# Two edits to a transformer kernel: the head norms' eps add goes from GpSimd to VectorE, and ScalarE writes the high halves of h's first two feature tiles from PSUM

## The chip, the cores and the metric

The kernel runs on one core of a Trainium2 chip. Five engines work side by side, each through its own list of instructions in the order in which they were issued: TensorE (PE, matrix products into the accumulators in PSUM), VectorE (DVE), ScalarE (ACT), GpSimd (POOL) and SyncE (SP, which starts the DMAs). An instruction that needs another engine's result waits for a semaphore, and everything behind it in its engine's list waits too. The metric is the device time of one execution in microseconds (us).

## The reference, cut to what matters

Two transformer models in a row run over 256 tokens of width 1024, two layers each. In the first, a layer is attention (stick-breaking in one, with a forget gate in the other) and a feed-forward net with a width-3 convolution. In the second, layer 0 is differential attention over the tokens and a context of 256 more, layer 1 a short convolution, each with a SwiGLU net. Between any two sub-layers stands the same pattern:

```python
x = x + gate * rmsnorm(o, g_post)             # first model; x + gate * o in the second
h = rmsnorm(x, g_pre) * (1.0 + scale) + shift
y = h @ w                                     # the next sub-layer's first products
```

and in the differential attention each head's queries, keys and outputs are normed once more:

```python
q = rmsnorm_2(q.reshape(bsz, -1, 2, DIFF_HEADS, HEAD_DIM_2), q_norm)
k = rmsnorm_2(k.reshape(bsz, -1, 2, DIFF_HEADS, HEAD_DIM_2), k_norm)
o = rmsnorm_2(o, subln) * (1.0 - lam_init)
# rmsnorm_2(x, g) = x * rsqrt(mean(x * x) + 1e-6) * g
```

## The kernel before, in words

All products are float32 made of pieces: a factor A is split into H (A rounded to the PE's fast float32 format) and L = A − H, and `mm3` makes each product of three matmuls, high·high, low·high and high·low. Weights stream from HBM in pieces of 128x1024; ScalarE casts each to `wh` and VectorE subtracts to get `wl`. The 256 tokens are two token tiles t of 128, the 1024 features eight feature tiles kt of 128.

At the end of each sub-layer stands a tail (`tail`, seven of them): for each t the residual `x` is updated, the row norm is taken (sums of squares on ScalarE into `junk`, the root `ssr` on GpSimd), `u` is the normed row block, and `put_ht` turns it into h with features on the partitions. `put_ht` transposes `u` on PE into two PSUM tiles named `tps` (128x512 each, one bank; kt 0 to 3 in the first, kt 4 to 7 in the second). Then, in the five steps (0), (1), (2,3), (4,5), (6,7), it makes `hf` = tps · scale + shift in SBUF, on VectorE for kt 0 to 3 and on ScalarE for kt 4 to 7; ScalarE casts `hf` to the high half (`h0h` for kt 0 to 3, `h1h` for kt 4 to 7), and VectorE subtracts to get the low half (`h0l`, `h1l`). `make_ctx` calls `put_ht` twice more for the context (`hc0h` and so on), so there are 16 calls.

The next sub-layer's first products take the halves of kt 0 first. After the four tails that lead to a SwiGLU or convolution net or to the short convolution these are the `fp` matmuls of `first_tiles` (EARLY = 2 output tiles f): for each t, for each f, for kt 0 to 7, three matmuls of 128x256. 24 matmuls make one f of one t; `fps` copies the result out, and the `gu` matmuls of the remaining output tiles follow. After the others they are `acc` or `kc` matmuls of 128x512.

No engine's list is written by hand. Class `Rec` records every operation, `Rec.schedule` sorts them with estimated costs, earliest first, and `emit` issues them (line 573, so every instruction of the trace carries that line). What an operation must wait for is set in `access`. For tiles in PSUM it adds one rule (lines 343 to 346):

```python
if t.psum and not write:
    for r in t.reads:
        if r.eng != op.eng:
            op.deps.setdefault(r, 1)
```

so of two engines that read the same PSUM tile, the one recorded later waits for the earlier.

`rstd` makes (ss + eps)^(−1/2) in two GpSimd instructions, `ms` and `rstd`. It is called 28 times, all in the differential attention: 12 times for eight heads at once (128x8, through `head_rstd`) and 16 times for one head's output (128x1; VectorE then scales that output to `on`). The row norms of the tails use other code.

Of the kernel before, what the change touches and what calls it, by code (L numbers as in the profile page):

```python
# [13 lines left out]
AF = mybir.ActivationFunctionType  # L14
ALU = mybir.AluOpType
# [13 lines left out]
EPS = 1e-6  # L29
# [582 lines left out]
class Builder:  # L612
# [165 lines left out]
    def rstd(self, ss, n=1):  # L778

        nc = self.nc  # L780
        t = self.sb.tile([P, 16], F32, tag="ms", name="ms")
        r = self.sb.tile([P, 16], F32, tag="rstd", name="rstd")
        nc.gpsimd.tensor_scalar(out=t[:, 0:n], in0=ss, scalar1=EPS, scalar2=None, op0=ALU.add)
        nc.gpsimd.tensor_tensor(out=r[:, 0:n], in0=t[:, 0:n], in1=self.mhalf[:, 0:n], op=ALU.pow)
        return r[:, 0:n]

# [41 lines left out]
    def put_ht(self, ht, xn, t, sc, sh):  # L828

        nc = self.nc  # L830
        src = {}
        for ks in self.BANKS:
            ps = self.pmm.tile([P, 4, P], F32, name="tps")
            for i, kt in enumerate(ks):
                nc.tensor.transpose(ps[:, i, :], xn[:, kt * P : (kt + 1) * P], self.eye)
                src[kt] = ps[:, i, :]
        for ks in self.STEPS:
            n, kt = len(ks), ks[0]
            h = self.sb.tile([P, n, P], F32, name="hf")
            for k in range(n):  # L840
                a, b = self.modcols[sc][:, kt + k : kt + k + 1], self.modcols[sh][:, kt + k : kt + k + 1]
                if kt + k in self.ON_DVE:
                    nc.vector.tensor_scalar(out=h[:, k, :], in0=src[kt + k], scalar1=a, scalar2=b, op0=ALU.mult, op1=ALU.add)
                else:
                    nc.scalar.activation(out=h[:, k, :], in_=src[kt + k], func=AF.Identity, scale=a, bias=b)
            k0 = kt % 4
            hh, hl = (z[:, t, k0 : k0 + n, :] for z in ht[kt // 4])
            nc.scalar.copy(hh, h)
            nc.vector.tensor_tensor(out=hl, in0=h, in1=hh.bitcast(F32), op=ALU.subtract)

    @staticmethod
# [839 lines left out]
```

## Time and profile before

| | us |
|---|---|
| median of 3 runs | 1337.94 |
| the runs' range | 1335.98 to 1338.98 |
| the profiled execution's own time | 1337.94 |
| its span, first to last instruction | 1335.9 |
| PE busy | 1301.9 (97%) |
| DVE busy | 1082.9 (81%) |
| ACT busy | 715.1 (54%) |
| POOL busy | 76.1 (6%) |

The span is the time from the first to the last instruction; 2.0 us of the execution lie outside it. Busy time counts how long an engine had an instruction at work; matmuls overlap one another, so the time that one costs is the distance between the starts of two neighbours. PEclk is the granted clock of TensorE as a share of the full 2.4 GHz.

### The profile page before, as it was taken

The numbers are of one execution on the slowest core, as the hardware profiler recorded it, in microseconds if no ns is written. First come the engines' busy times: TensorE is split into PE (matmuls) and PEld (weight loads), VectorE is DVE, ScalarE is ACT, GpSimd is POOL, SyncE is SP. The second block draws the span as 40 slices with busy tenths as digits, with TensorE's granted clock in tenths as the row PEclk, the third lists the DMA queues.
The fourth block names the chain that finished last, engine by engine and source line by source line (L and its number), as shares of the span: only waits on it lengthen the run. The fifth ranks groups of instructions, "written<-read, shape, count | busy, mean of one in ns | idle before, by whom it ended". The sixth has DMA issues, their size and how long they took to land.

```text
span 1335.9 us, 21951 instructions
## 1 busy us (share of the span) xinstructions
PE 1301.9 (97%) x8760; PEld 1172.1 (88%) x8760; DVE 1082.9 (81%) x1827; ACT 715.1 (54%) x1249; POOL 76.1 (6%) x102
## 2 busy tenths in 40 slices
PE   5999999999999999999999999899999999999998
PEld 4888799999898799999888777799999999999997
DVE  6899898998999699999799988876766998855542
ACT  3565755555666664556543667644444635644430
POOL 0000100000100000001033123100000000000000
PEclk9999999999999999999999999899999999999999
DMA  9866678887666357777454533577776587555520
GB/s 360 310 254 261 239 292 318 319 327 300 227 251 256 122 190 266 270 278 266 158 205 150 212 132 118 192 287 278 259 281 252 221 315 284 194 187 187 189 96 32
DMA packets 45319, 311.82 MB, mean 233 GB/s; under 512 B 5280, under 2 KB 5664, under 8 KB 8864
## 3 DMA queue, kind: packets, MB, share of 16 engines
q1 hardware_dynamic: 45216, 310.42, 62.4%
q8 instruction: 68, 1.11, 0.3%
q14 instruction: 35, 0.29, 0.1%
HBM read 309.35 MB, written 1.05 MB: 232 GB/s over the span
## 4 chain that ended last, share of the span: by engine, by line
PE 85%; DVE 6%; ACT 3%; issue 2%; DMA 1%; POOL 1%; SPq 0%; ACTq 0%; POOLq 0%; DVEq 0%
PE gu L573 34%; PE acc L573 28%; PE qkps L573 6%; PE fp L573 4%; PE cu L573 3%; DVE w L573 2%; PE bb L573 2%; PE qps L573 2%; PE z L573 2%; PE tps L573 1%; DMA w<-in_wst_dram 1%; PE op L573 1%; DVE wl L573 1%; PE kc L573 1%; PE atp L573 1%
## 5 line engine op out<-in xcount | busy, mean ns | idle before, releaser
L573 DVE TENSOR_TENSOR wl<-w,wh 128x1024 fp32r<-128x1024 f32 x392 | 470.5, 1220 | 71.5 <-ACT wh L573 47.9
L573 ACT CAST wh<-w 128x1024 fp32r<-128x1024 f32 x392 | 402.4, 1049 | 94.3 <-DMA w<-in_wst_dram 56.8
L573 DVE CUSTOM_DVE_ANT_0 w<-w,rows,vec 128x1024 f32<-128x1024 f32 x192 | 242.3, 1278 | 12.1 <-DMA w<-in_wst_dram 11.8
L573 PE MATMUL gu<-h1h,wh 128*128 128x256 f32 x640 | 181.3, 283 | 0.0
L573 PE MATMUL gu<-h1h,wl 128*128 128x256 f32 x640 | 181.2, 283 | 0.0
L573 PE MATMUL gu<-h0h,wl 128*128 128x256 f32 x640 | 181.1, 283 | 0.0
L573 PE MATMUL gu<-h1l,wh 128*128 128x256 f32 x640 | 181.1, 283 | 0.0
L573 PE MATMUL gu<-h0l,wh 128*128 128x256 f32 x640 | 181.1, 283 | 0.0
L573 PE MATMUL gu<-h0h,wh 128*128 128x256 f32 x640 | 180.9, 283 | 0.0
L573 PE MATMUL acc<-wh,yh 128*128 128x512 f32 x352 | 137.6, 392 | 0.0
L573 PE MATMUL acc<-wl,yh 128*128 128x512 f32 x352 | 137.4, 391 | 0.0
L573 PE MATMUL acc<-wh,yl 128*128 128x512 f32 x352 | 135.3, 389 | 0.0
L573 PEld LDWEIGHTS gu<-h0l,wh 128*128 128x128 f32 x640 | 122.6, 192 | 2.2
L573 PEld LDWEIGHTS gu<-h0h,wh 128*128 128x128 f32 x640 | 122.5, 192 | 2.3
L573 PEld LDWEIGHTS gu<-h1l,wh 128*128 128x128 f32 x640 | 122.8, 192 | 0.1
L573 PEld LDWEIGHTS gu<-h1h,wh 128*128 128x128 f32 x640 | 122.8, 192 | 0.1
L573 PEld LDWEIGHTS gu<-h1h,wl 128*128 128x128 f32 x640 | 122.8, 192 | 0.0
L573 PEld LDWEIGHTS gu<-h0h,wl 128*128 128x128 f32 x640 | 122.6, 192 | 0.0
L573 DVE TENSOR_TENSOR y<-s,gu 128x256 f32<-128x256 f32 x80 | 33.5, 418 | 74.6 <-ACT s L573 74.5
L573 ACT ACTIVATE s<-gu 128x256 f32<-128x256 f32 x40 | 15.4, 385 | 137.3 <-PE gu L573 137.3
L573 PEld LDWEIGHTS acc<-wh,yl 128*128 128x128 f32 x352 | 66.1, 188 | 14.3
L573 PEld LDWEIGHTS acc<-wh,yh 128*128 128x128 f32 x352 | 66.4, 189 | 12.2 <-ACT yh L573 0.2
(364 smaller groups left out, 2662.9 us busy)
## 6 DMA issues: line engine op xcount, KB each, us to landing
w<-in_wst_dram SPq DMA_DIRECT2D x284, 1024.0 KB, 4.9
w<-in_wst_dram SPq DMA_DIRECT2D x16, 512.0 KB, 11.4
x<-in_x_dram SPq DMA_DIRECT2D x2, 512.0 KB, 6.1
cx<-in_ctx_dram SPq DMA_DIRECT2D x2, 512.0 KB, 6.7
out_dram<-x SPq DMA_DIRECT2D x1, 512.0 KB, 2.6
out_dram<-x SPq DMA_DIRECT2D x2, 256.0 KB, 2.0
cst<-in_consts_dram SPq DMA_DIRECT2D x1, 264.0 KB, 5.5
smalls<-in_smalls_dram SPq DMA_DIRECT2D x1, 256.0 KB, 5.0
```

What stands on the lines that cost most here:

```text
L573: fn(*[real(a) for a in op.args], **{k: real(v) for k, v in op.kw.items()})
```

## The change

Two edits. In `rstd` the add of eps is issued on VectorE and only the power stays on GpSimd. In `put_ht`, for the steps of one feature tile (kt 0 and kt 1), ScalarE no longer casts `hf` from SBUF; it computes scale · tps + shift itself from the PSUM tile and writes the high half. VectorE still computes `hf` from the same PSUM tile and still subtracts.

```diff
@@ def rstd(self, ss, n=1):
-        nc.gpsimd.tensor_scalar(out=t[:, 0:n], in0=ss, scalar1=EPS, scalar2=None, op0=ALU.add)
+        nc.vector.tensor_scalar(out=t[:, 0:n], in0=ss, scalar1=EPS, scalar2=None, op0=ALU.add)
         nc.gpsimd.tensor_tensor(out=r[:, 0:n], in0=t[:, 0:n], in1=self.mhalf[:, 0:n], op=ALU.pow)
@@ def put_ht(self, ht, xn, t, sc, sh):
             hh, hl = (z[:, t, k0 : k0 + n, :] for z in ht[kt // 4])
-            nc.scalar.copy(hh, h)
+            if n == 1:
+                nc.scalar.activation(out=hh[:, 0, :], in_=src[kt], func=AF.Identity, scale=a, bias=b)
+            else:
+                nc.scalar.copy(hh, h)
             nc.vector.tensor_tensor(out=hl, in0=h, in1=hh.bitcast(F32), op=ALU.subtract)
```

28 instructions go from GpSimd to VectorE, and 32 ScalarE instructions (16 calls, two steps each) read another tile. The sorting moves others with them. The first tail of the program, from the first attention to the first convolution net, shows how. VectorE there, token tile 0, before; `acc` holds the sub-layer's output, `rows` the gate, and a number behind a name tells one tile from the next:

```order
L573 TENSOR_TENSOR u_1534<-acc_1259,rows_955 128x512
L573 TENSOR_SCALAR hf_1545<-tps_1529,msc_f_1488,msh_f_926 128x128 [waits PE_49]
L573 TENSOR_SCALAR hf_1549<-tps_1529,msc_f_1488,msh_f_926 128x128
L573 TENSOR_SCALAR hf_1553<-tps_1529,msc_f_1488,msh_f_926 128x128
L573 TENSOR_TENSOR h0l_1556<-hf_1545,h0h_1551 128x128 [waits Activation_49]
L573 TENSOR_TENSOR h0l_1556<-hf_1549,h0h_1551 128x128 [waits Activation_49]
L573 TENSOR_SCALAR hf_1553<-tps_1529,msc_f_1488,msh_f_926 128x128
L573 TENSOR_TENSOR u_1534<-acc_1388,rows_955 128x512
L573 TENSOR_TENSOR h1l_1574<-hf_1547,h1h_1570 128x256 [waits Activation_49]
L573 TENSOR_TENSOR h0l_1556<-hf_1553,h0h_1551 128x256 [waits Activation_49]
L573 SCALAR_TENSOR_TENSOR x_25_89<-u_1534,ssr_1538,x_25_89 128x512 [waits Pool_49]
L573 TENSOR_TENSOR h1l_1574<-hf_1563,h1h_1570 128x256 [waits Activation_49]
```

The reads of `tps` for kt 0, 1 and 2 stand in a row here, and `u` and `x` behind them. VectorE at the same place, after the change:

```order
L573 TENSOR_TENSOR u_1534<-acc_1259,rows_955 128x512
L573 TENSOR_SCALAR hf_1545<-tps_1529,msc_f_1488,msh_f_926 128x128 [waits PE_49]
L573 TENSOR_TENSOR u_1534<-acc_1388,rows_955 128x512
L573 SCALAR_TENSOR_TENSOR x_25_89<-u_1534,ssr_1538,x_25_89 128x512 [waits DVE_49,Pool_49]
L573 TENSOR_TENSOR h0l_1559<-hf_1545,h0h_1550 128x128 [waits Activation_49]
L573 TENSOR_SCALAR hf_1563<-tps_1529,msc_f_1488,msh_f_926 128x128
L573 TENSOR_TENSOR h1l_1567<-hf_1547,h1h_1561 128x256 [waits Activation_49]
L573 SCALAR_TENSOR_TENSOR x_25_89<-u_1534,ssr_1538,x_25_89 128x512 [waits DVE_49]
L573 TENSOR_TENSOR h0l_1559<-hf_1563,h0h_1550 128x128 [waits Activation_49]
L573 TENSOR_SCALAR hf_1578<-tps_1529,msc_f_1488,msh_f_926 128x128 x2
L573 TENSOR_TENSOR h1l_1567<-hf_1556,h1h_1561 128x256 [waits Activation_49]
L573 TENSOR_TENSOR wl_1584<-w_346_1454,wh_1527 128x1024 [waits DMAHW4_49]
```

The three reads no longer stand in a row; each of kt 0 and kt 1 is followed by its `h0l`, which waits for ScalarE, and parts of `u`, `x` and `h1l` stand between them. ScalarE at the same place, before, from the first read of the second PSUM tile:

```order
L573 ACTIVATE hf_1547<-tps_1540,msh_f_926,msc_f_1488 128x128 [waits PE_49]
L573 CAST h0h_1551<-hf_1545 128x128 [waits DVE_49]
L573 CAST h0h_1551<-hf_1549 128x128 [waits DVE_49]
L573 ACTIVATE hf_1547<-tps_1540,msh_f_926,msc_f_1488 128x128
L573 ACTIVATE hf_1563<-tps_1540,msh_f_926,msc_f_1488 128x128
L573 CAST h1h_1570<-hf_1547 128x256 [waits Activation_49]
L573 CAST h0h_1551<-hf_1553 128x256 [waits DVE_49]
```

The two casts for kt 0 and kt 1 are neighbours and read `hf` in SBUF. ScalarE, after:

```order
L573 ACTIVATE hf_1547<-tps_1540,msh_f_926,msc_f_1488 128x128 [waits PE_49]
L573 ACTIVATE h0h_1550<-tps_1529,msh_f_926,msc_f_1488 128x128 [waits DVE_49]
L573 ACTIVATE hf_1547<-tps_1540,msh_f_926,msc_f_1488 128x128
L573 ACTIVATE hf_1556<-tps_1540,msh_f_926,msc_f_1488 128x128 [waits Activation_49]
L573 CAST h1h_1561<-hf_1547 128x256 [waits Activation_49]
L573 ACTIVATE hf_1556<-tps_1540,msh_f_926,msc_f_1488 128x128
L573 ACTIVATE h0h_1550<-tps_1529,msh_f_926,msc_f_1488 128x128 [waits DVE_49]
```

In their place two `h0h` activations read `tps`; they stand five places apart, each waits for VectorE, and the first casts and `hf` activations of kt 4 to 7 stand between them. TensorE, before, near the end of token tile 0's second f (names `wh` and `wl` are the weight halves, `eye` the identity that transposes):

```order
L573 MATMUL fp_1559<-wh_1599,h1l_1574 128x256
L573 MATMUL fp_1559<-wh_1599,h1h_1570 128x256
L573 MATMUL tps_1636<-eye_85,u_1534 128x128 x4
L573 MATMUL tps_1645<-eye_85,u_1534 128x128 x4
L573 MATMUL fp_1559<-wl_1608,h1h_1570 128x256
L573 MATMUL fp_1559<-wh_1599,h1l_1574 128x256
```

The eight transposes of token tile 1 stand here with five of token tile 0's 48 matmuls behind them. TensorE, after, at the transposes of the same token tile 1, now in the first f:

```order
L573 MATMUL fp_1554<-wh_1480,h0h_1550 128x256
L573 MATMUL fp_1554<-wl_1503,h0h_1550 128x256
L573 MATMUL fp_1554<-wh_1480,h0l_1559 128x256
L573 MATMUL tps_1599<-eye_85,u_1534 128x128 x4
L573 MATMUL tps_1608<-eye_85,u_1534 128x128 x4
L573 MATMUL fp_1554<-wh_1505,h1h_1561 128x256
L573 MATMUL fp_1554<-wl_1514,h1h_1561 128x256
```

The transposes moved to behind kt 3 of the first f, with 36 of token tile 0's matmuls behind them.

## Rows read from the trace of the kernel before

**Rows 1.** The page: busy time, share and count of each engine; the chain of work that ended last, by engine.

```profile
PE 1301.9 (97%) x8760; PEld 1172.1 (88%) x8760; DVE 1082.9 (81%) x1827; ACT 715.1 (54%) x1249; POOL 76.1 (6%) x102
...
PE 85%; DVE 6%; ACT 3%; issue 2%; DMA 1%; POOL 1%; SPq 0%; ACTq 0%; POOLq 0%; DVEq 0%
```

**Rows 2.** Stretches of the span (us from its start), with their length, and then the busy time (and count of instructions) of PE, the weight loads PEld, DVE, ACT and POOL, the granted clock, the DMA engines' share and GB/s. The stretches hold the tails: the first one, the one to the second layer's values, the one to the second convolution net, and the one behind the differential attention (two).

```profile
140.00:150.00 10.00, 7.67 (x36) 6.18 (x36) 9.56 (x21) 7.50 (x18) 1.97 (x2) 0.84 0.48 188
150.00:160.00 10.00, 9.04 (x68) 8.11 (x67) 9.37 (x17) 8.48 (x17) 1.78 (x2) 0.99 0.41 121
340.00:352.00 12.00, 12.00 (x66) 10.24 (x65) 11.83 (x27) 8.17 (x21) 1.97 (x2) 1.00 0.58 212
...
466.00:476.00 10.00, 9.39 (x76) 8.76 (x76) 9.13 (x18) 10.00 (x22) 0.55 (x1) 1.00 0.46 161
...
840.00:850.00 10.00, 6.45 (x32) 5.07 (x30) 10.00 (x17) 6.51 (x11) 2.02 (x2) 0.82 0.44 167
850.00:860.00 10.00, 9.35 (x56) 9.35 (x57) 8.11 (x21) 6.73 (x19) 0.00 (x0) 0.67 0.29 107
```

**Rows 3.** The timeline of the first tail, token tile 0: start, length, engine, line, operation and tiles; x2 or x3 are so many in a row, with their joint length.

```profile
144.71 0.68 DVE L573 TENSOR_TENSOR u<-acc,rows 128x512 f32<-128x512 f32 x1
...
145.31 1.04 DVE L573 TENSOR_SCALAR hf<-tps,msc_f,msh_f 128x128 f32<-128x128 f32 x3
145.57 0.46 ACT L573 ACTIVATE hf<-tps,msh_f,msc_f 128x128 f32<-128x128 f32 x1 [0.99 <-PE tps L573]
145.93 0.48 ACT L573 CAST h0h<-hf 128x128 fp32r<-128x128 f32 x2
146.26 0.48 DVE L573 TENSOR_TENSOR h0l<-hf,h0h 128x128 fp32r<-128x128 f32 x2
...
147.31 0.41 ACT L573 CAST h0h<-hf 128x256 fp32r<-128x256 f32 x1
...
147.92 0.41 DVE L573 TENSOR_TENSOR h0l<-hf,h0h 128x256 fp32r<-128x256 f32 x1
...
148.25 0.74 DVE L573 SCALAR_TENSOR_TENSOR x<-u,ssr,x 128x512 f32<-128x512 f32 x1
...
148.77 0.42 PE L573 MATMUL fp<-wh,h0h 128*128 128x256 f32 x1
...
148.98 0.41 PE L573 MATMUL fp<-wl,h0h 128*128 128x256 f32 x1
...
149.91 2.35 DVE L573 TENSOR_TENSOR wl<-w,wh 128x1024 fp32r<-128x1024 f32 x2
150.02 1.06 ACT L573 ACTIVATE junk<-x 128x1025 bf16<-128x1025 f32 x1 [0.56 <-DVE x L573]
...
151.25 1.42 POOL L573 TENSOR_TENSOR ssr<-ss,mhalf 128x1 f32<-128x1 f32 x1 [5.83 <-ACT junk L573]
```

**Rows 4.** The timeline of the same tail, token tile 1.

```profile
152.71 1.00 DVE L573 TENSOR_SCALAR u<-x,ssr 128x512 f32<-128x512 f32 x2 [0.45 <-POOL ssr L573]
...
153.46 1.06 PE L573 MATMUL tps<-eye,u 128*128 128x128 f32 x8
...
154.76 1.04 DVE L573 TENSOR_SCALAR hf<-tps,msc_f,msh_f 128x128 f32<-128x128 f32 x3
...
157.91 0.41 DVE L573 TENSOR_TENSOR h0l<-hf,h0h 128x256 fp32r<-128x256 f32 x1
...
158.38 0.39 PE L573 MATMUL fp<-wh,h0l 128*128 128x256 f32 x1
...
158.60 0.28 PE L573 MATMUL fp<-wh,h0h 128*128 128x256 f32 x1
...
158.72 0.28 PE L573 MATMUL fp<-wl,h0h 128*128 128x256 f32 x1
```

**Rows 5.** All instructions that touch `hf`: count, shortest, median and longest in ns, first and last start, shapes.

```profile
L573 ACT CAST h0h<-hf x46: 286/302/413, 16.1 to 1149.8; 128x128 fp32r<-128x128 f32 x28, 128x256 fp32r<-128x256 f32 x18
L573 DVE TENSOR_TENSOR h0l<-hf,h0h x46: 274/292/426, 16.5 to 1150.2; 128x128 fp32r<-128x128 f32 x28, 128x256 fp32r<-128x256 f32 x18
...
L573 DVE TENSOR_SCALAR hf<-tps,msc_f,msh_f x32: 394/402/411, 145.3 to 1149.2; 128x128 f32<-128x128 f32 x32
L573 ACT ACTIVATE hf<-tps,msh_f,msc_f x32: 448/458/470, 145.6 to 1150.7; 128x128 f32<-128x128 f32 x32
```

**Rows 6.** The timeline at the `h0l` of kt 2 and 3, token tile 1, in four later tails: to the second layer's values (and there the first of PE's matmuls behind those of kt 2), to the second convolution net, to the short convolution, behind it.

```profile
353.77 0.42 DVE L573 TENSOR_TENSOR h0l<-hf,h0h 128x256 fp32r<-128x256 f32 x1
...
357.25 0.39 PE L573 MATMUL acc<-wh,h0h 128*128 128x512 f32 x1
...
475.50 0.43 DVE L573 TENSOR_TENSOR h0l<-hf,h0h 128x256 fp32r<-128x256 f32 x1 [0.24 <-ACT h0h L573]
...
1055.06 0.42 DVE L573 TENSOR_TENSOR h0l<-hf,h0h 128x256 fp32r<-128x256 f32 x1
...
1150.18 0.43 DVE L573 TENSOR_TENSOR h0l<-hf,h0h 128x256 fp32r<-128x256 f32 x1 [0.20 <-ACT h0h L573]
```

**Rows 7.** The instructions that touch `ms`, in the 128x1 form: count, shortest, median and longest in ns, first and last start.

```profile
L573 POOL TENSOR_SCALAR ms<-oss x16: 223/302/1097, 764.7 to 835.2; 128x1 f32<-128x1 f32 x16
```

**Rows 8.** Who waited for an instruction that touches `rstd`, and for how long (us, times).

```profile
  DVE on L573: 5.8, 9
...
  PE dop L573: 1.3, 3
```

## The prediction

> **What bounds the kernel now.** I read the page first. TensorE is busy for 1301.9 of 1335.9 us, and 85% of the chain that ended last is TensorE, 6% VectorE, 3% ScalarE [rows 1]. So only time in which TensorE stands still, or runs at a lower clock, can change much; a microsecond more on VectorE costs nothing wherever TensorE has other products to do. The windows then show where it does stand still: in the tails, where one sub-layer has ended and the next needs h. In the first tail it is busy for 7.67 and 9.04 of two times 10 us, behind the differential attention for 6.45 and 9.35; in the tail to the second layer's values it does not stand still at all, in the others it waits little (9.39 of 10 us in one of them) [rows 2]. VectorE is at 9 to 10 of 10 us in the same windows, so it has no slack there.
>
> The timelines show the tail from near. For token tile 0, VectorE makes three `hf` in a row, 0.32 us from one to the next; ScalarE meanwhile reads the other bank; its two casts follow at 145.93, the first `h0l` at 146.26, and the `h0l` of kt 2 and 3 ends at 148.33 [rows 3]. From first `hf` to that end: 3.0 us. For token tile 1 it is 154.76 to 158.32, 3.6 us, and the third matmul of kt 2, which needs this `h0l`, starts at 158.38 [rows 4]. So the last link of the chain is VectorE's `h0l`, and TensorE hangs on it directly.
>
> **The change, part by part.** The profiled execution took 1337.94 us, which is its span of 1335.9 and 2.0 around it, and it is also the median; the sum is made against it.
>
> *ScalarE's H from the bank.* On its own the edit takes a cast of 302 ns and puts an activation in its place; ScalarE's `hf` of the same shape took 458 [rows 5]. That is 0.16 us more for ScalarE, 32 times, 5 us in all on an engine that is half idle. What is meant to go is the step `hf` before the cast. But the order shows `h0h` still waiting for VectorE: both read the same `tps`, and `access` lets two engines read one PSUM tile only after one another. So the wait stays, 0.40 us of `hf` and then 0.46 of `h0h` [rows 5]. Worse, the rule binds in the other direction too: VectorE's next `hf` must wait until ScalarE has read. Where VectorE read three times in a row, bank 0 now passes to and fro: VectorE kt 0, ScalarE kt 0, VectorE kt 1, ScalarE kt 1, VectorE kt 2 and 3. And in the gaps the sorting has put other work of VectorE, which now stands in front of the next link.
>
> The Trainium skill bears on this, in PSUM — Partial Sum Buffer, section "PSUM bank collisions raise a hardware error": two engines must not be in one bank (and the same quarter of the partitions) at once, two readers included. Rows 3 agree as far as they go: VectorE's `hf` from 145.31 and ScalarE's from 145.57 overlap, in two different banks. By this rule the serial chain is not a whim of `access` that the chip could overrun; without it H could be ready 0.4 us earlier per token tile.
>
> First tail, token tile 0, laid along the new order with the durations of [rows 3, 5]: `hf` 145.31 to 145.71; the second `u` (0.68) to 146.31; `x` (0.74) to 147.05; `h0l` of kt 0 (0.28) to 147.3; `hf` of kt 1 (0.40) to 147.7; `h1l` (0.42) to 148.1; the second `x` (0.74) to 148.8; `h0l` of kt 1 to 149.1; two `hf` (0.72) to 149.8; `h1l` to 150.2; a `wl` (2.35 / 2 = 1.18) to 151.4, while ScalarE does `junk` (1.06) and the cast of kt 2 and 3 (0.41); `h0l` to 151.9. That is 6.6 us instead of 3.0. TensorE can do kt 0 and 1 meanwhile and then stands. Token tile 1's `x` is ready at 148.8, where before `junk` on it began at 150.02, and that is used up in part: `ssr` (1.42) follows `junk` and is done at about 151.6, `u` runs from 151.9 to 152.9 (before, 152.71 to 153.71 [rows 4]).
>
> Token tile 1 in the new order is `wl`, `hf`, `wl`, `h0l`, `hf`, `h1l`, `wl`, `h0l`, two `hf`, `h1l`, `wl`, `h0l`. From the first `hf`: 0.40 + 1.18 + 0.28 + 0.40 + 0.42 + 1.18 + 0.28 + 0.72 + 0.42 + 1.18 + 0.42 = 6.9 us instead of 3.6; three `wl` make the difference. With `hf` at 154.25 and about 0.7 for ScalarE being late (its own weight casts stand between), `h0l` ends at 161.9 instead of 158.32. The third matmul of kt 2 moves from 158.38 to 162.0 (+3.6). In front of it stand six `gu` matmuls that had come later, at 0.12 us each [rows 4] 0.7 us. So **+2.9 us** in this tail. What stood still in token tile 0 is contained in it, since TensorE waits for this last link in any case; the 36 matmuls behind the moved transposes (36 × 0.12 = 4.3 us) end before it.
>
> The other tails are laid in the same way; before, `h0l` of kt 2 and 3 of token tile 1 ended at 354.19, 475.93, 1055.48 and 1150.61 [rows 6].
> - To the values: the products are 512 wide and cover more. TensorE was done with kt 2 at 357.25 [rows 6]; I get 359.1: **+1.9**.
> - To the second convolution net: 479.4 instead of 475.9, less nine `gu` matmuls drawn forward (1.1): **+2.4**.
> - To the short convolution: 1058.8 instead of 1055.5, less 0.8: **+2.5**.
> - Behind the short convolution: 42 matmuls of token tile 0 stand behind the transposes; the last `fp` ends 3.5 us later, less 0.4: **+3.1**.
> - To the differential attention: the context's key products are there to do, **+0.5**; behind it, where both token tiles' transposes come before the products in either order and the clock is down already (0.82, 0.67 [rows 2]), **+0.9**. The two context calls have 45 us until they are needed: 0.
>
> Sum: 2.9 + 1.9 + 2.4 + 2.5 + 3.1 + 0.5 + 0.9 = 14.2 us. If TensorE finds twice the cover that I gave it, half is left, 7; if none, 3.3 to 3.6 in each of five tails and 1.4 in the other two, 19.
>
> *The norms' eps.* 28 adds leave GpSimd (median 302 ns in the 128x1 form) [rows 7]. On VectorE no such add is in the trace; the nearest rows for a small one bound it by 0.07 us (the distance between two 128x1 instructions) and 0.16 us (a 128x8 multiply), so 2 to 4.5 us of VectorE, which is at nine tenths in that stretch. What it can give back is VectorE's wait for `rstd`, 5.8 us in 9 waits [rows 8], shortened by up to 0.3 each, 2.7. What it can cost: the add waits on VectorE for ScalarE's `ojunk`, in front of work that did not have to wait, up to the full 16 × 0.3 = 5 us. Bounds −3 and +5; TensorE has other products there and I take 0.
>
> *The clock.* Where TensorE stands still for some microseconds, it runs slower afterwards: in the first tail the products from 148.77 stand 0.21 us apart instead of 0.12 [rows 3, 4], at a granted clock of 0.84 over the window, and behind the differential attention at 0.82 and 0.67 [rows 2], that is in part at 1.2 instead of 2.4 GHz. 0.84 over 10 us is 1.6 us, the other two together 5.1. The longer waits may bring this to other tails: 0 to +6, not in the sum.
>
> Forecast: 1337.9 + 14.2 = **1352 us**.
>
> **The rivals.**
> *Covered.* TensorE's list has enough in front of the late products that only part of the lengthened chain shows: half of the sum, 1345. For it: the windows in which TensorE never waited [rows 2]; against it: in the first tail the matmul follows `h0l` after 0.06 us [rows 4], there is no slack to eat.
> *Clock.* Three more tails fall to the lower level, 1.6 to 2.5 us each on top: 1358. For it: the two tails with waits have it already; against it: waits of 0.5 us elsewhere did not bring it (1.00 in the other windows).
> *Norms first, not slower.* The saved add on GpSimd shortens the wait for `rstd` at most heads (9 × 0.3 = 2.7 us), and the lengthened chain lies wholly under products: 1335. It decides if TensorE's wait for `h0h` and `h0l` does not grow in any tail. Against it: only 1.3 us of TensorE's time hung on `rstd` [rows 8], so even a full saving hardly arrives.
> *The edit does what it says.* H comes straight from the bank beside VectorE's read, and is 0.4 us earlier for 14 token tiles, of which TensorE waited in a few: 1335 to 1337. The order excludes it, since `h0h` waits for VectorE.
>
> **How the numbers follow.** The serial chain 0.57 (1347 to 1356), covered 0.19 (1341 to 1347), clock 0.12 (1356 to 1364), norms or H early 0.06 (1333 to 1335), and 0.06 that all cancels within 0.2%, 2.7 us, about what a measurement here can tell from no change. So faster 0.06, same 0.06, slower 0.88. The range 1341 to 1362 leaves out the last two and the far end of the clock.
>
> **What would show it.** In the profile after: VectorE's `hf` for kt 0, 1 and 2 no longer in a row, ScalarE's `h0h` from `tps` after each; first `hf` to last `h0l` 6 to 7 us; TensorE's waits in the tails for `h0h` and `h0l` up by 2 to 3 us each, for `u` in the first tail too; `ms` gone from GpSimd with `on` as late as before. The forecast is wrong if the first tail's third matmul of kt 2 starts before 160, or if the tails cost under 1 us each; then the cover was larger than I laid it. It is also wrong if the time between 670 and 840 us grows by more than 3 us: then the norms' adds are what costs.

## The result and the profile after

The changed kernel takes 1350.78 us (median of 4 runs, 1349.92 to 1351.90); the kernel before, on the same chip, 1338.16. The ratio is 1.0095 with a 95% interval of 1.008 to 1.011: slower by 12.6 us. The profiled execution took 1350.14 us, with a span of 1348.4.

The page has these lines in place of [rows 1]:

```profile
PE 1307.9 (97%) x8760; PEld 1174.9 (87%) x8760; DVE 1085.3 (80%) x1855; ACT 722.3 (54%) x1249; POOL 65.0 (5%) x74
...
PE 86%; DVE 9%; ACT 3%; POOL 1%; issue 1%; DMA 0%; SPq 0%; ACTq 0%; POOLq 0%; DVEq 0%
```

TensorE's share is still 97%; in the chain of work that ended last VectorE's part has grown from 6% to 9%. The windows (columns as in [rows 2]; the last two hold the tails to and behind the short convolution, which now lie 5 to 9 us later):

```profile
140.00:150.00 10.00, 6.44 (x28) 4.48 (x26) 9.56 (x20) 7.92 (x19) 2.03 (x3) 0.85 0.51 197
150.00:160.00 10.00, 9.42 (x52) 8.93 (x53) 8.23 (x16) 6.75 (x13) 2.10 (x2) 0.64 0.39 114
1048.00:1060.00 12.00, 9.32 (x51) 8.56 (x50) 10.71 (x26) 8.77 (x22) 0.55 (x1) 0.72 0.40 150
1150.00:1158.00 8.00, 5.05 (x24) 4.45 (x25) 6.45 (x15) 6.44 (x17) 0.55 (x1) 0.79 0.33 119
```

In the first tail TensorE's busy time fell from 7.67 to 6.44 of 10 us, and the granted clock over the next 10 us is 0.64 instead of 0.99; the last two windows, at 0.72 and 0.79, lie in tails whose clock had been full. Before, these two tails read:

```profile
1040.00:1060.00 20.00, 18.95 (x143) 17.55 (x143) 19.31 (x38) 12.03 (x27) 1.66 (x1) 1.00 0.51 189
1138.00:1160.00 22.00, 21.34 (x169) 20.25 (x168) 17.49 (x34) 15.52 (x34) 1.17 (x1) 1.00 0.52 203
```

The stretches of the three tails in which the clock is at its lower level (0.50, that is 1.2 of 2.4 GHz) after the change:

```profile
147.00:157.20 10.20, 8.51 (x33) 7.21 (x33) 8.86 (x19) 7.60 (x17) 2.17 (x2) 0.50 0.30 98
1051.60:1058.30 6.70, 6.13 (x27) 5.84 (x28) 5.86 (x15) 3.47 (x10) 0.16 (x1) 0.50 0.48 170
1154.00:1157.20 3.20, 2.98 (x14) 2.98 (x15) 2.35 (x5) 1.64 (x5) 0.00 (x0) 0.50 0.14 23
```

Before, there was one such stretch in these tails, from 146.8 to 150.0 in the first.

The timeline of the first tail, token tile 0, answers to [rows 3]:

```profile
145.49 0.40 DVE L573 TENSOR_SCALAR hf<-tps,msc_f,msh_f 128x128 f32<-128x128 f32 x1
...
145.80 0.68 DVE L573 TENSOR_TENSOR u<-acc,rows 128x512 f32<-128x512 f32 x1
146.11 0.45 ACT L573 ACTIVATE h0h<-tps,msh_f,msc_f 128x128 fp32r<-128x128 f32 x1
146.40 0.74 DVE L573 SCALAR_TENSOR_TENSOR x<-u,ssr,x 128x512 f32<-128x512 f32 x1
...
147.06 0.28 DVE L573 TENSOR_TENSOR h0l<-hf,h0h 128x128 fp32r<-128x128 f32 x1
...
147.26 0.41 DVE L573 TENSOR_SCALAR hf<-tps,msc_f,msh_f 128x128 f32<-128x128 f32 x1
...
147.79 0.47 ACT L573 ACTIVATE h0h<-tps,msh_f,msc_f 128x128 fp32r<-128x128 f32 x1
147.93 0.74 DVE L573 SCALAR_TENSOR_TENSOR x<-u,ssr,x 128x512 f32<-128x512 f32 x1
...
150.90 0.42 DVE L573 TENSOR_TENSOR h0l<-hf,h0h 128x256 fp32r<-128x256 f32 x1
...
151.76 1.01 DVE L573 TENSOR_SCALAR u<-x,ssr 128x512 f32<-128x512 f32 x2 [0.44 <-POOL ssr L573]
```

`hf` of kt 0 and of kt 1 stand 1.77 us apart (before: 0.32), with `u`, `x` and `h0l` between them; from the first `hf` to the end of the last `h0l` it is 5.8 us instead of 3.0. Token tile 1, in place of [rows 4]:

```profile
152.52 1.94 PE L573 MATMUL tps<-eye,u 128*128 128x128 f32 x8
...
153.82 0.40 DVE L573 TENSOR_SCALAR hf<-tps,msc_f,msh_f 128x128 f32<-128x128 f32 x1
...
161.08 0.42 DVE L573 TENSOR_TENSOR h0l<-hf,h0h 128x256 fp32r<-128x256 f32 x1
...
161.87 0.28 PE L573 MATMUL gu<-h0h,wl 128*128 128x256 f32 x1
...
161.99 0.28 PE L573 MATMUL fp<-wh,h0l 128*128 128x256 f32 x1
```

Here it is 7.7 us instead of 3.6, and the third matmul of kt 2 starts at 161.99 instead of 158.38. TensorE did not wait for that `h0l`, though: it was there at 161.50, and the matmuls in front of the third one stand 0.12 us apart. TensorE came late, because it had stood still in token tile 0 and had then worked at the lower level until 157.2; the eight transposes alone took 1.94 us instead of 1.06. TensorE's waits over the whole execution (us in total, times, longest):

```profile
PE fp L573 <- ACT h0h L573: 6.4, 9, 1.7
...
PE fp L573 <- DVE h0l L573: 1.4, 3, 0.7
```

Before, these two lines were 4.1 us and 0.2 us. In the first tail and in the two at the short convolution, the three dear ones, all these waits now lie in token tile 0, none in token tile 1. At the short convolution as well TensorE reads token tile 1's last `h0l` of kt 2 and 3 only after it is there: ready at 1063.05 and read at 1064.56 in the tail to it, 1160.73 and 1162.56 in the tail behind it. In the tail to the short convolution a single one of these waits is 1.68 us long, at kt 1 of token tile 0:

```profile
1051.53 0.58 PE L573 MATMUL fp<-wh,h0h 128*128 128x256 f32 x1 [1.68 <-ACT h0h L573]
```

To see where the 12.5 us of the span came in, I took matmuls that stand at the same place of the program in both traces (the first transpose of a tail, the last `gu` of a net, and so on) and their starts or ends. The differences of the offset from one place to the next are what each stretch cost; they add up to the span's difference; what the table leaves out, 0.2 us and less at a place, lies ahead of the first tail and between the stretches.

| stretch | forecast | whole change | put_ht's edit alone | eps edit alone |
|---|---|---|---|---|
| first tail and its net | +2.9 | +2.6 | +2.4 | 0.0 |
| tail to the second layer's values | +1.9 | +0.8 | +0.7 | 0.0 |
| tail to the second convolution net | +2.4 | +0.7 | +0.7 | 0.0 |
| tail to the differential attention | +0.5 | +0.6 | +0.5 | 0.0 |
| norms, heads, and the tail behind them | +0.9 | −0.3 | −2.3 | +5.9 |
| tail to the short convolution | +2.5 | +4.1 | +4.1 | 0.0 |
| tail behind it | +3.1 | +3.7 | +3.8 | 0.0 |

### The profile page after: what moved, and what is told of

Same layout as the page of the kernel before. It is cut to its first block, busy times and chain, and to the rows that moved or that the text cites. A ratio compares the mean times of both kernels' runs of the same rounds, so it can differ in the third digit from the quotient of the medians.

```text
span 1348.4 us, 21931 instructions
## 1 busy us (share of the span) xinstructions
PE 1307.9 (97%) x8760; PEld 1174.9 (87%) x8760; DVE 1085.3 (80%) x1855; ACT 722.3 (54%) x1249; POOL 65.0 (5%) x74
## 3 DMA queue, kind: packets, MB, share of 16 engines
HBM read 309.35 MB, written 1.05 MB: 230 GB/s over the span
## 4 chain that ended last, share of the span: by engine, by line
PE 86%; DVE 9%; ACT 3%; POOL 1%; issue 1%; DMA 0%; SPq 0%; ACTq 0%; POOLq 0%; DVEq 0%
PE gu L573 34%; PE acc L573 28%; PE qkps L573 7%; PE fp L573 4%; PE cu L573 3%; DVE w L573 2%; PE bb L573 2%; DVE wl L573 2%; PE z L573 2%; PE qps L573 1%; PE tps L573 1%; DVE p L573 1%; DVE dmx L573 1%; PE op L573 1%; PE atp L573 1%
```

## The experiments

There are two theories to test. Theory 1: the edit of `put_ht` costs because VectorE and ScalarE now read one PSUM tile in turns, and the eps edit costs nothing. Theory 2 came with the first run: the eps edit has a cost of its own. The median of the kernel before in these runs lies between 1337.5 and 1338.6 us; ratios are against it.

**Each edit alone.**

```diff
@@ def rstd, the eps edit alone
-        nc.gpsimd.tensor_scalar(out=t[:, 0:n], in0=ss, scalar1=EPS, scalar2=None, op0=ALU.add)
+        nc.vector.tensor_scalar(out=t[:, 0:n], in0=ss, scalar1=EPS, scalar2=None, op0=ALU.add)
```

> Only the eps add goes to VectorE; put_ht is as before. Theory 1 (the shared PSUM tile costs it all): 1337 to 1339 us, no change that can be told. Rival (the adds on a VectorE that is nine tenths busy cost a good part of the 12.6 us): 1342 or more. Rival (the shorter chain to rstd gains, and hid a larger loss of the other edit): 1334 or less.

Measured: 1343.09 us, ratio 1.0039 (1.0025 to 1.0052). The rival holds: the adds cost 4.5 to 5 us by themselves, all of it in the stretch of the differential attention.

The other half alone is the changed kernel with that line as before.

> Only ScalarE's H from the PSUM tile for kt 0 and 1; eps stays on GpSimd. Theory 1: 1349 to 1352 us, the time of the whole change. Rival (eps adds): 1346 or less.

Measured: 1347.21 us, ratio 1.0069 (1.0056 to 1.0081). Missed by 2 us on the low side. Some 9 us belong to `put_ht`; the whole change is 3.6 us above this run.

**A PSUM tile of its own for ScalarE.**

```diff
@@ def put_ht, on top of its edit
+        twin = self.pmm.tile([P, 2, P], F32, name="tpz")
+        for kt in range(2):
+            nc.tensor.transpose(twin[:, kt, :], xn[:, kt * P : (kt + 1) * P], self.eye)
...
-                nc.scalar.activation(out=hh[:, 0, :], in_=src[kt], func=AF.Identity, scale=a, bias=b)
+                nc.scalar.activation(out=hh[:, 0, :], in_=twin[:, kt, :], func=AF.Identity, scale=a, bias=b)
```

> Only the edit of put_ht, and PE transposes kt 0 and 1 a second time into a PSUM tile of its own, which ScalarE alone reads; two more transposes per call (0.13 us each on PE). Theory 1 (the shared tile is the cause): 1336 to 1340 us, ScalarE's h0h beside VectorE's hf. Rival (ScalarE's activation from PSUM is itself slower than the cast, 0.16 us in 32 places, and sits on the chain): 1341 to 1344. Rival (any other order of the tail costs as much): 1348 or more.

Measured: 1338.12 us, ratio 0.9998 (0.9989 to 1.0006). In its first tail:

```profile
145.56 1.35 DVE L573 TENSOR_SCALAR hf<-tps,msc_f,msh_f 128x128 f32<-128x128 f32 x4
...
146.18 0.80 ACT L573 ACTIVATE h0h<-tpz,msh_f,msc_f 128x128 fp32r<-128x128 f32 x2
...
146.83 0.48 DVE L573 TENSOR_TENSOR h0l<-hf,h0h 128x128 fp32r<-128x128 f32 x2
```

VectorE's four `hf` stand in a row again, and ScalarE's two `h0h` (0.80 us) run beside them. The three dear tails (the first and the two at the short convolution) cost −0.1, +0.1 and −0.4 us here, against 2.4, 4.1 and 3.8. So the shared tile is shown to be the cause of the cost in these tails. The total is a sum of more: with its 32 more transposes this run costs 1.7 us in the tail to the second layer's values, and it gains 2.4 from the norms to the tail behind the heads. In this form, where ScalarE's read need not wait for VectorE's, the edit gains nothing that can be told: H, made from the second transposes, is no earlier than from a cast of 0.30 us behind `hf`.

**Less other work between the links.** The same instructions and waits, but the sorting counts the `h0h` activation as 1 ns with no handover, so that it sees no gap to fill.

```diff
@@ def lag
+        if d.quick or op.quick:
+            return 0.0
...
@@ def put_ht
                 nc.scalar.activation(out=hh[:, 0, :], in_=src[kt], func=AF.Identity, scale=a, bias=b)
+                self.nc.ops[-1].quick, self.nc.ops[-1].cost = True, 1.0
```

> As the run before (only the edit of put_ht), the same operations and the same waits, but the sorting is told that the h0h activations take no time, so that it puts less of VectorE's other work between two links of the chain (in the first tail one x instead of two x, an h1l and a wl). Theory 1a (the pieces of other work in the gaps are most of the cost): 1339 to 1343 us. Theory 1b (the passing of the bank to and fro itself is most of it): 1346 to 1351.

Measured: 1352.92 us, ratio 1.0115 (1.0096 to 1.0134): dearer than the edit itself, and above both theories. The five executions lie between 1350.2 and 1356.5 us. By stretches of the trace the three dear tails cost 3.9, 4.2 and 1.9 us, 10.0 in sum against the edit's 10.3; what is dearer are the tails to the values and to the second convolution net, 1.6 and 2.2. In the first tail, token tile 0 and then token tile 1:

```profile
149.59 0.42 DVE L575 TENSOR_TENSOR h0l<-hf,h0h 128x256 fp32r<-128x256 f32 x1
...
149.93 0.74 DVE L575 SCALAR_TENSOR_TENSOR x<-u,ssr,x 128x512 f32<-128x512 f32 x1
...
153.38 1.00 DVE L575 TENSOR_SCALAR u<-x,ssr 128x512 f32<-128x512 f32 x2 [0.44 <-POOL ssr L575]
```

```profile
156.38 0.41 DVE L575 TENSOR_SCALAR hf<-tps,msc_f,msh_f 128x128 f32<-128x128 f32 x1 [0.87 <-PE tps L575]
...
162.23 0.42 DVE L575 TENSOR_TENSOR h0l<-hf,h0h 128x256 fp32r<-128x256 f32 x1
```

The chain did become shorter, 4.4 us (from 145.61) instead of 5.8 and 6.3 instead of 7.7. But token tile 1's `x` now ran at 149.93, behind the chain, instead of 147.93; `u` followed at 153.38 instead of 151.76, and the shorter chain ended at 162.65 instead of 161.50. So my picture of needless pieces in the chain fell. As I read it, they are work that the tail needs anyway, and on a full VectorE either the chain waits or what it pushes back; no run here shows that by itself, since this one moves other work too.

**The tile handed over once.** VectorE's four reads recorded first, ScalarE's two behind; or ScalarE's two first.

```diff
@@ def put_ht, ScalarE first
         for ks in self.STEPS:
+            if len(ks) == 1:
+                kt = ks[0]
+                a, b = self.modcols[sc][:, kt : kt + 1], self.modcols[sh][:, kt : kt + 1]
+                nc.scalar.activation(out=ht[kt // 4][0][:, t, kt % 4, :], in_=src[kt], func=AF.Identity, scale=a, bias=b)
+        for ks in self.STEPS:
             n, kt = len(ks), ks[0]
...
-            if n == 1:
-                nc.scalar.activation(out=hh[:, 0, :], in_=src[kt], func=AF.Identity, scale=a, bias=b)
-            else:
+            if n > 1:
                 nc.scalar.copy(hh, h)
```

> Only the edit of put_ht, with ScalarE's two h0h recorded first: the tile passes from ScalarE to VectorE once, and H does not wait for VectorE. Theory 1: 1337 to 1342 us; H some 0.3 us earlier than before, the first h0l 0.4 later. Rival (what counts is the last h0l, and VectorE has pushed u and x in front of hf by then): 1344 to 1350.

Measured: 1339.58 us, ratio 1.0016 (1.0006 to 1.0027), inside theory 1's range. In the first tail:

```profile
145.36 0.81 ACT L573 ACTIVATE h0h<-tps,msh_f,msc_f 128x128 fp32r<-128x128 f32 x2 [0.55 <-PE tps L573]
...
146.13 0.74 DVE L573 SCALAR_TENSOR_TENSOR x<-u,ssr,x 128x512 f32<-128x512 f32 x1
146.79 0.73 DVE L573 TENSOR_SCALAR hf<-tps,msc_f,msh_f 128x128 f32<-128x128 f32 x2
...
147.77 0.39 PE L573 MATMUL fp<-wh,h0l 128*128 128x256 f32 x1 [1.39 <-DVE h0l L573]
```

H is ready from 145.82, while VectorE, kept from the bank until 146.2, has `x` in front of `hf`; TensorE then waits 1.39 us for `h0l`. The three dear tails cost 1.4, 2.2 and 0.8 us, 4.4 in sum against 10.3. The total is that low because this order also gains 3.5 us from the norms to the tail behind the heads, which theory 1 had not counted.

The other order puts the loop over VectorE's `hf` of kt 0 to 3 ahead of all else in `put_ht`:

```diff
@@ def put_ht, VectorE first
+        for own in (True, False):
             for ks in self.STEPS:
...
+                if (kt in self.ON_DVE) != own:
+                    continue
...
+            for ks in self.STEPS:
...
                 if n == 1:
                     nc.scalar.activation(out=hh[:, 0, :], in_=src[kt], func=AF.Identity, scale=a, bias=b)
```

> Only the edit of put_ht, with VectorE's four hf recorded first and ScalarE's two h0h behind them: the shared PSUM tile passes from VectorE to ScalarE once instead of to and fro. Theory 1 (passing to and fro is the cost): 1338 to 1342 us; the first h0h comes 1 us later than before, which may show in the tails without cover. Rival (H behind a read of the bank is late in any order): 1346 or more.

Measured: 1353.49 us, ratio 1.0115 (1.0099 to 1.013): missed by far. The stretches tell two things apart. The three dear tails cost 3.6, 2.6 and 1.3 us, 7.5 in sum, less than the 10.3 of the turns and more than the 4.4 of ScalarE first. About 8 us more came in the second convolution net, far from the tails; TensorE's waits from 485 to 600 us:

```profile
PE acc L573 <- ACT yh L573: 2.9, 3, 1.5
PE gu L573 <- ACT wh L573: 1.0, 1, 1.0
```

Neither wait is there in the kernel before. The sorting, once nudged, had changed the order there too: half of the context's transposes came at 587.9, still inside the net, where they had stood at 602 behind it. Why `yh` came late is not shown; right before it ScalarE stood idle for VectorE's `y` (1.05 us at 531.35, 1.06 at 570.26). So the total says little on the tails, and the rule of thumb "one handover is cheap" holds for one of the two orders alone.

**The eps adds.** In the run with the eps edit alone, the last heads read so:

```profile
836.78 0.20 ACT L573 ACTIVATION_READ_ACCUMULATOR ojunk<-dop 128x1 f32 x1
...
837.33 1.22 DVE L573 TENSOR_TENSOR wl<-w,wh 128x1024 fp32r<-128x1024 f32 x1
...
838.46 0.15 DVE L573 TENSOR_SCALAR ms<-oss 128x1 f32<-128x1 f32 x1
...
838.69 1.46 POOL L573 TENSOR_TENSOR rstd<-ms,mhalf 128x1 f32<-128x1 f32 x1 [1.66 <-DVE ms L573]
...
840.18 0.35 DVE L573 TENSOR_SCALAR on<-dop,rstd 128x128 f32<-128x128 f32 x1 [0.44 <-POOL rstd L573]
...
840.59 0.33 PE L573 MATMUL dop<-eye,on 128*128 128x128 f32 x1 [0.50 <-DVE on L573]
```

`ojunk`'s sum is there at 836.98; `ms`, 0.15 us long, starts only at 838.46, behind a `wl` of 1.22. `on` follows at 840.18, 3.2 us after the sum, and TensorE waited for it. This is the last but one of the 16 heads; the last one before reads:

```profile
834.89 0.19 ACT L573 ACTIVATION_READ_ACCUMULATOR ojunk<-dop 128x1 f32 x1
834.98 2.35 DVE L573 TENSOR_TENSOR wl<-w,wh 128x1024 fp32r<-128x1024 f32 x2
...
835.17 1.10 POOL L573 TENSOR_SCALAR ms<-oss 128x1 f32<-128x1 f32 x1 [0.50 <-ACT ojunk L573]
...
837.79 0.35 DVE L573 TENSOR_SCALAR on<-dop,rstd 128x128 f32<-128x128 f32 x1 [0.46 <-POOL rstd L573]
```

There GpSimd starts `ms` 0.09 us after the sum (835.08), though it takes 1.10, while VectorE is busy with `wl`; `on` comes after 2.7 (2.7 at the last but one as well). Over the 16 heads the mean from the sum to `on` is 1.99 us before and 3.29 with VectorE's add; `ms` starts after 0.13 and after 1.02.

Which of the 28 adds cost? Only the 16 of 128x1, or only the 12 of 128x8, went to VectorE:

```diff
-        nc.gpsimd.tensor_scalar(out=t[:, 0:n], in0=ss, scalar1=EPS, scalar2=None, op0=ALU.add)
+        (nc.vector if n == 1 else nc.gpsimd).tensor_scalar(out=t[:, 0:n], in0=ss, scalar1=EPS, scalar2=None, op0=ALU.add)
```

> put_ht as before; only the 16 one-head adds (128x1, between ojunk and on) go to VectorE, the 12 eight-head adds stay on GpSimd. Theory 2 (the wait of ms in VectorE's list on each head's chain is the cost): 1341 to 1344 us, most of the 4.5. Rival (the eight-head adds, which stand on the way to the queries and keys): 1336 to 1339.

> put_ht as before; only the 12 eight-head adds go to VectorE. Theory 2: 1336 to 1340 us, since the sum of squares that they follow is VectorE's own and they stand right behind it. Rival: 1341 to 1344.

Measured: 1341.52 us, ratio 1.0034 (1.0021 to 1.0047), and 1336.31, 0.9993 (0.9983 to 1.0002). The one-head adds are the cost; the eight-head ones, behind VectorE's own sum, are free.

ScalarE for all 28 adds, and no add at all:

```diff
-        nc.gpsimd.tensor_scalar(out=t[:, 0:n], in0=ss, scalar1=EPS, scalar2=None, op0=ALU.add)
+        nc.scalar.activation(out=t[:, 0:n], in_=ss, func=AF.Identity, scale=1.0, bias=self.epsc)
```

(`epsc` is a column that holds eps.)

> put_ht as before; the eps add of the 28 norms goes to ScalarE instead of VectorE, where it stands behind ojunk, whose result it needs. Theory 2 (in the run with VectorE's add alone ms began 1.02 us after ojunk instead of 0.13, because it stands in VectorE's full list, and on began 1.3 us later; that is the 4.5 us): 1336 to 1340 us. Rival (each handover to GpSimd costs, whichever engine adds; or the add lengthens any full engine's list): 1341 to 1345.

> put_ht as before; the 28 norms leave out eps (the add of 1e-6 to the mean square is not done), so neither GpSimd nor VectorE adds. Theory 2 (the latency from ojunk to on matters): 1333 to 1337 us, since rstd begins 0.4 us earlier at 16 heads. Rival (only the order counts, latency of a few tenths is covered): 1337 to 1340.

Measured: 1339.50 us, ratio 1.0009 (1.0000 to 1.0018), and 1336.45, 0.9993 (0.9984 to 1.0001). With no add the gain cannot be told from none: before, the add was covered.

ScalarE for the one-head adds and VectorE for the others:

```diff
+        if n == 1:
+            nc.scalar.activation(out=t[:, 0:n], in_=ss, func=AF.Identity, scale=1.0, bias=self.epsc)
+        else:
+            nc.vector.tensor_scalar(out=t[:, 0:n], in0=ss, scalar1=EPS, scalar2=None, op0=ALU.add)
```

> put_ht as before; each eps add on the engine that made its input, so that it stands right behind it: the 16 one-head adds on ScalarE behind ojunk, the 12 eight-head adds on VectorE behind the sum of squares. Theory 2 (an add costs what it waits in its engine's list, and GpSimd's add takes 0.46 us that the other two do in less): 1334 to 1337 us, a little faster than before and than the run with ScalarE for all 28. Rival (only the order's accidents move the time by 2 us in either direction): 1337 to 1341.

Measured: 1344.94 us, ratio 1.0049 (1.0035 to 1.0064). A clear miss, and the trace says why:

```profile
830.37 0.19 ACT L573 ACTIVATION_READ_ACCUMULATOR ojunk<-dop 128x1 f32 x1
...
831.40 0.78 ACT L573 ACTIVATE p<-dz,dnb,rq 128x512 f32<-128x512 f32 x1
...
832.16 0.77 ACT L573 ACTIVATE p<-dz,dnb,rq 128x512 f32<-128x512 f32 x1
...
832.92 0.29 ACT L573 ACTIVATE ms<-oss,epsc 128x1 f32<-128x1 f32 x1
...
841.65 0.40 PE L573 MATMUL dop<-eye,on 128*128 128x128 f32 x1 [2.87 <-DVE on L573]
```

The add does not always stand right behind `ojunk`: here the sum was there at 830.56, a `wh` cast and two `p` activations stood between, and `ms` began at 832.92. Later TensorE waited 2.87 us for an `on`. I had put the engine in place of the position in its list; the sorting decides the second.

Both edits with the own tile:

> Both edits, with the PSUM tile of its own for ScalarE's reads. If the two costs are separate and add: the eps adds' 4 to 5 us on top of the run with the own tile, 1341 to 1344 us. If they share a cause (VectorE's list in general), less: 1338 to 1340.

Measured: 1339.49 us, ratio 1.0016 (1.0008 to 1.0025). The adds cost 1.4 us here by the medians and 2.4 by the ratios, less than the 4.5 to 5 alone. Set side by side, the runs that differ in the adds alone fall into two groups by one number, the mean from `ojunk`'s sum to `on` over the 16 heads:

| run | sum to `on`, us | ratio |
|---|---|---|
| no add | 1.75 | 0.9993 |
| eight-head adds on VectorE | 1.97 | 0.9993 |
| before | 1.99 | 1 |
| all on ScalarE | 2.31 | 1.0009 |
| one-head on ScalarE, eight-head on VectorE | 2.89 | 1.0049 |
| all on VectorE | 3.29 | 1.0039 |
| one-head adds on VectorE | 3.30 | 1.0034 |

Up to 2.3 us the time is that of before within 0.1%, from 2.9 it is 0.3 to 0.5% longer; inside the second group the number does not order the runs, so it is not the whole cause. With `put_ht`'s edit it goes from 2.06 to 2.98 us (1.0069 to 1.0095), with the own tile from 2.06 to 3.00 (0.9998 to 1.0016). No version beat the kernel before beyond what can be told.

## Why the prediction was right, and where it was wrong

The time, 1352 forecast and 1350.8 measured, and the direction were right, and so was the rule that makes the larger part. On which path TensorE then lost its time the prediction was wrong. Point by point:

- *ScalarE's read must wait for VectorE's, and VectorE's next for ScalarE's.* Right; the own tile takes the cost of the three dear tails away. The Trainium skill's rule, in PSUM — Partial Sum Buffer, section "PSUM bank collisions raise a hardware error", that two engines must not be in one bank at once, readers included, is what makes the turns necessary; no run here let them overlap.
- *First tail.* 6.6 us laid and 5.8 measured for token tile 0, 7.6 and 7.7 for token tile 1: VectorE's chain is right. The third matmul of kt 2 at 162.0 and 161.99, and +2.9 and +2.6, agree in part by luck. "TensorE waits for this last link in any case" did not hold in the three dear tails: its waits came in token tile 0, which I had taken as contained in token tile 1's, and it came to token tile 1's last `h0l` 0.5 to 1.8 us after that was ready. So the sign "waits up by 2 to 3 us each" failed too: the two lines of waits grew by 3.5 us over the whole execution.
- *The other tails.* (Five of the seven tails lead to `fp` matmuls, not the four named ahead: `fp` has 80 of each kind, 16 a tail.) Their sum without the one behind the heads, 10.4 forecast and 9.9 measured, came out by errors that cancel: the two tails in the middle cost about a third of what I laid (+1.5 instead of +4.3), and those to and behind the short convolution were dearer (+7.8 instead of +5.6). There token tile 0 cost, with a wait of 1.68 us at its kt 1 in the tail to it, and the clock.
- *The norms' eps: 0.* This is the term that was furthest off: about 5 us alone, at the end of its bounds of −3 and +5, and 3.6 on top of the other edit. "TensorE has other products there" was wrong; TensorE is full on the whole, yet the last heads' chain lies open at the end. The price I named for the other side has that size, but it ran the other way round: I had VectorE's other work held up while the add waits for `ojunk`; in the run with the eps edit alone the add waited behind VectorE's other work, 1.02 us on the mean, and no wait of VectorE for `ojunk` is listed. VectorE's wait for `rstd` did shrink, from 5.8 to 4.0 us, and bought nothing. "`on` as late as before" was wrong: 2.98 us after the sum in the changed kernel, 1.99 before.
- *The tail behind the heads: +0.9.* Wrong in sign. With the heads before it, it gained 2.3 us in the run with `put_ht`'s edit alone, and about as much with the own tile (2.4), the eight-head adds on VectorE (2.4) and no add (2.3). Why all these orders of that stretch are better than the one before is open.
- *Clock.* It did fall in the two tails at the short convolution, as the rival had it, and in the first it stayed down for 10 us instead of 3. What that costs depends on what TensorE has to do then. In the first tail the run with `put_ht`'s edit alone has TensorE's instructions in the same order as the changed kernel; its clock was down for 6.8 us, from 147.4 to 154.2, and it costs +2.4 instead of +2.6. The kernel before and the run with the eps edit alone share one order there as well; in the second the clock stayed at 1.00, and the two do not differ (0.0). But in the run without an add this same order had its fall at 160.3, where TensorE had products to do, and that cost 1.5 us. At the short convolution TensorE worked on at the lower level without a wait: against the distances at the full clock its transposes and products stood some 2.4 us further apart in the tail to it and 1.3 us behind it. The last `h0l` was ready 1.5 and 1.8 us before TensorE read it, so my estimate is that at the full clock these tails would have been shorter by at least 1.5 and 1.3 us. Then some 3 of their +7.8 us are the clock's, and the chain's own part is about 5, near the 5.6 laid. No run here has these two tails in one order at both levels.

So 14 us were forecast for `put_ht`, without the clock, against 9 with some 3 of the clock in them, and 0 for the adds against 4. That the sum was nearer than its parts is luck.

## What to carry to other kernels

Before a reader of a PSUM tile is moved to another engine, look at who else reads that tile: two readers on different engines take turns, and a tile that went to one engine in a row then goes to and fro. A short instruction can cost what it waits in its engine's list rather than its length; a 0.15 us add on a full VectorE was done later than a 0.30 us add on an idle GpSimd. And where a planner sorts the lists, ask of each edit what it moves far away, and split the cost by stretches before a total is believed.

## What was not expected of the hardware

The add itself stayed within its bounds on VectorE, 0.15 us for 128x1 and 0.16 for 128x8:

```profile
L573 DVE TENSOR_SCALAR ms<-oss x16: 144/148/153, 771.2 to 842.0; 128x1 f32<-128x1 f32 x16
L573 DVE TENSOR_SCALAR ms<-ss x12: 159/164/172, 680.2 to 745.3; 128x8 f32<-128x8 f32 x12
```

GpSimd's, with a median near 0.3 us but up to 1.1 [rows 7], depends on what VectorE does at the same time. Of the 28 adds before, the six of 0.7 us and more lay for 0.6 to 1.2 us beside a `wl` or a custom `w` of VectorE (1.10 us at 835.17, beside two `wl`), while those beside its `dmx`, at 764.67 and 800.49, took 0.23 and 0.22. On the mean GpSimd was still the quicker way. That in one order of the first tail 3.4 us at the lower clock cost nothing in one execution and 1.5 us in another was new to me as well.
